# Gate and up of a feed-forward layer made together, a quarter of their products by Strassen's scheme

## The chip, the cores and the metric

The kernel runs on one core of a Trainium2 chip. Its time is the device time of one execution in microseconds (us), and three runs of the kernel before gave a median of 1607.12 us (1605.46 to 1607.89). The core has a matrix engine (TensorE, PE in the profile, with its weight loads shown apart as PEld), a vector engine (VectorE, DVE), a scalar engine (ScalarE, ACT), a general engine (GpSimd, POOL) and a queue engine (SyncE, SP) that issues the transfers. Matrix products are summed in eight PSUM banks of 128 x 512 fp32.

## The reference

One encoder layer on 256 tokens of 2048 features, all in fp32. The stages after the token mixers are

```
h   = layer_norm(ALPHA * h + m @ w_o, ln1_g, ln1_b)
gt, up = split(h @ w_gu, 2)                    # w_gu: 2048 x (2 x 5632)
ffn = (silu(gt) * up) @ w_down                 # w_down: 5632 x 2048
ple = sigmoid(h @ w_pg + b_pg) * (p @ w_pu)
out = layer_norm(ALPHA * h + ffn + ple, ln2_g, ln2_b)
```

Before them stand a first layer norm, one wide projection `h @ w_in`, a gated linear attention over four heads (GLA), a gated spatial mix and the gates that merge the two.

## The kernel before

Every fp32 product is made of three products of fp32r operands: a matrix is split into `hi` (a copy rounded to fp32r, ScalarE, L147) and `lo` (the rest, `raw - hi`, VectorE, L148), and `mm3` (L188 to L190) multiplies xh·wh, xl·wh and xh·wl into one bank. The activations are the stationary operand (128 features x 128 tokens), the weights the moving one (128 features x 512 columns).

The work is one stream of weight chunks. A chunk is two k-tiles (2 x 128 rows) of 512 columns, 512 KB. `pump` walks the stream: before chunk c is used, chunks up to c+5 are loaded and up to c+3 are split, then the chunk's matmuls are issued, then one waiting job (an evacuation or a transposition) is run. A `token_block` makes one block of 512 output columns for both token tiles (2 x 128 tokens) in two banks of the pool `pacc`. A chunk costs 12 matmuls: two k-tiles, two token tiles, three products. Each engine works in order, so a split that is late holds everything behind it on its engine.

In the feed-forward stage 11 gate blocks (`gt`) and 11 up blocks (`up`) alternate, with 8 chunks each. The gate's evacuation is a Silu on ScalarE (L858), the up's a multiplication on VectorE (L868); the result is transposed on TensorE (L282, tile `atp`) and split (L290, L291) to become the stationary operand of the down product. Gate and up come in three parts of 4, 4 and 3 blocks; behind each part stand four down blocks (`dn`) over the part's features, so the last has 12 k-tiles. That last down block is held: the first token tile is finished first, all weights being kept, so that its layer norm (L909, L912, `ln2_out`) can run beside the second tile's matmuls, which are made in two halves of 256 columns.

SBUF is shared by fixed pools: raw chunks, `hi` and `lo` have 4 buffers each (`wp`), eight large slots of 16 KB per partition hold streams and transposed activations (`big`), 7 small tiles (`t2`) the evacuations. PSUM gives 4 banks to blocks (`pacc`) and 4 to transpositions and attention (`paux`).

Of the kernel before, what the change touches and what calls it, by code (L numbers as in the profile page):

```python
# [28 lines left out]
KC = 2  # L29
ET = mybir.EngineType  # L30
# [8 lines left out]
def block_kernel(ctx: ExitStack, tc: tile.TileContext, x, p, ln0_g, ln0_b, w_in, b_in, w_f2, b_f2,  # L39
# [15 lines left out]
    wp = ctx.enter_context(tc.tile_pool(name="wp", bufs=2))  # L55
    big = ctx.enter_context(tc.tile_pool(name="big", bufs=8))
    tmp = ctx.enter_context(tc.tile_pool(name="tmp", bufs=4))
    sm = ctx.enter_context(tc.tile_pool(name="sm", bufs=4))
    pacc = ctx.enter_context(tc.tile_pool(name="pacc", bufs=4, space=bass.MemoryType.PSUM))
    paux = ctx.enter_context(tc.tile_pool(name="paux", bufs=4, space=bass.MemoryType.PSUM))  # L60

    def slot(name, dt=F32):
        return big.tile([P, 4096], dt, tag="big", name=name)

    def t2(name):
        return tmp.tile([P, CB], F32, tag="t2", name=name, bufs=7)

    def tr(name):
        return tmp.tile([P, CB], F32R, tag="t2", name=name, bufs=7)
# [3 lines left out]

    def bcast(src, c0, name, n=CB):
        t = tmp.tile([P, CB], F32, tag="bc", name=name, bufs=4)
        nc.sync.dma_start(t[:, :n], src[c0:c0 + n].partition_broadcast(P))
        return t

# [1 line left out]
    xs = slot("xs").rearrange("p (t d) -> p t d", t=NT)  # L80
    for t in range(NT):
        for c in range(D // XC):
            nc.sync.dma_start(xs[:, t, c * XC:(c + 1) * XC],
                              x[t * P:(t + 1) * P, c * XC:(c + 1) * XC])
# [8 lines left out]
    # vectors that are needed with features on partitions: rows of 128, turned over at once  # L93
# [26 lines left out]
    chunks = []  # L120

    def add_chunk(src, nk, nc_, consume, dst=None):
        chunks.append([src, nk, nc_, consume, None, None, dst])

    G = {}
    jobs = deque()

# [5 lines left out]
    def load(c):  # L133
        src, nk, ncol = chunks[c][:3]
        raw = wp.tile([P, KC * CB], F32, tag="raw", name=f"raw{c}", bufs=4)
        nc.sync.dma_start(raw[:, :nk * ncol].rearrange("p (k c) -> p k c", k=nk), src)
        chunks[c][4] = raw

    def split(c):
        n = chunks[c][1] * chunks[c][2]  # L140
        raw = chunks[c][4]
        if chunks[c][6] is None:
            hi = wp.tile([P, KC * CB], F32R, tag="hi", name=f"hi{c}", bufs=4)
            lo = wp.tile([P, KC * CB], F32R, tag="lo", name=f"lo{c}", bufs=4)
        else:
            hi, lo = chunks[c][6]()
        nc.scalar.activation(hi[:, :n], raw[:, :n], AF.Copy)  # L147
        nc.vector.tensor_tensor(out=lo[:, :n], in0=raw[:, :n], in1=hi[:, :n].bitcast(F32),  # L148
                                op=ALU.subtract)
        chunks[c][5] = (hi, lo)  # L150

    state = {"load": 0, "split": 0, "use": 0}

    def ahead(nload, nsplit):
        while state["load"] < min(nload, len(chunks)):
            load(state["load"])
            state["load"] += 1
        while state["split"] < min(nsplit, len(chunks), state["load"]):
            split(state["split"])
            state["split"] += 1  # L160
# [9 lines left out]
    def consume(c):  # L170
        chunks[c][3](*chunks[c][5])
        state["use"] = c + 1

    def pump(upto=None):
        end = len(chunks) if upto is None else upto
# [16 lines left out]
    def token_block(src, nk, xT, evac, name, held=None, halves=False):  # L192
        """[tokens, CB] = xT.T @ W; evac(t, psum) after the last k. Over the chunks in held the
        first token tile runs ahead of the second, which reads the kept weights. With halves the
        second is finished in two column halves (only with all chunks held)."""
# [4 lines left out]
        def one(i, n, t, c0=0, c1=CB, ps=None):  # L200
            hi, lo = st["w"][i]
            ps = st["ps"][t] if ps is None else ps
            xh, xl = xT() if callable(xT) else xT
            for k in range(n):
                kk = i * KC + k
                xo = kk * S + t * P
                mm3(ps[:, c0:c1], xh[:, xo:xo + P], xl[:, xo:xo + P],
                    hi[:, k * CB + c0:k * CB + c1], lo[:, k * CB + c0:k * CB + c1],
                    kk == 0, kk == nk - 1)
# [4 lines left out]
        def dst(i):  # L214
            def get():
                j = (i - h0_) % 4
                if j == 0:
                    st["keep"] = (slot(f"{name}_kh{i}", F32R), slot(f"{name}_kl{i}", F32R))
                return tuple(x[:, j * KC * CB:(j + 1) * KC * CB] for x in st["keep"])
            return get  # L220

        def mk(i):
            def consume(hi, lo):
                if i == 0:
                    st["ps"] = [pacc.tile([P, CB], F32, tag="acc", name=f"{name}_{t}")
                                for t in range(NT)]
# [11 lines left out]
                elif i == h1_ - 1 and halves:  # L238
                    for j in range(2):
                        ps = st["ps"][1] if j == 0 else pacc.tile([P, CB], F32, tag="acc",  # L240
                                                                  name=f"{name}_1b")
# [9 lines left out]
        for i in range(nchunk):  # L251
            add_chunk(src[:, i * KC:i * KC + size(i), :], size(i), CB, mk(i),
                      dst(i) if h0_ <= i < h1_ else None)

# [1 line left out]
    def rstd_of(var, n, name, eps_scale=None):  # L256
        """(var * scale + eps) ** -0.5 for [P, n]."""
# [27 lines left out]
    def split_to(src, xT, k0, t, eng=nc.vector):  # L285
        xh, xl = xT
        oh = xh.rearrange("p (k s) -> p k s", s=S)[:, k0:k0 + 4, t * P:(t + 1) * P]
        ol = xl.rearrange("p (k s) -> p k s", s=S)[:, k0:k0 + 4, t * P:(t + 1) * P]
# [18 lines left out]
    def ln_turn(src, xT, t, c, key, name):  # L307
        """Normalised rows (t, 512 features from c) to xT with gain and bias."""
        ps = transpose4(src[:, t, c * CB:(c + 1) * CB], f"{name}_ps{t}_{c}")
# [3 lines left out]
    def pair_ps(src, k0, name):  # L313
        """Both token tiles, features of k0 and k0 + 1."""
        ps = aux(f"{name}_ps{k0}")
        for i in range(2):
            for t in range(NT):
                nc.tensor.transpose(ps[:, i * S + t * P:i * S + (t + 1) * P],
                                    src[:, t, (k0 + i) * P:(k0 + i + 1) * P], ident)
# [9 lines left out]
    def pair_split(a, xT, k0):  # L329
        xh, xl = xT  # L330
        sl = slice(k0 * S, (k0 + 2) * S)
        nc.scalar.activation(xh[:, sl], a, AF.Copy)
        nc.vector.tensor_tensor(out=xl[:, sl], in0=a, in1=xh[:, sl].bitcast(F32), op=ALU.subtract)
# [6 lines left out]
    def residual(g, b, c, name):  # L340
        """Gain and bias of the token-major copy, 512 features."""
        gt = bcast(g, c * CB, f"{name}g{c}")
        bt = bcast(b, c * CB, f"{name}b{c}")
        for t in range(NT):
            y = h0[:, t, c * CB:(c + 1) * CB]
# [4 lines left out]
    h0 = xs  # L350
    h0T = (slot("h0Th", F32R), slot("h0Tl", F32R))
# [7 lines left out]
    def keep_busy(n, name):  # L359
        """TensorE's clock rises only while it works."""  # L360
# [12 lines left out]
    def ws_job():  # L373
# [7 lines left out]
        # rows j of chunk 1 do not reach positions i of chunk 0  # L381
# [5 lines left out]
    def v_evac(b):  # L387
        def evac(t, ps):
# [581 lines left out]
```

## Time and profile before

| | before |
|---|---|
| median of three runs | 1607.12 us |
| the profiled execution's span, first to last instruction | 1606.5 us |
| TensorE busy, instructions | 1583.1 us, 7520 |
| VectorE busy | 929.4 us |
| ScalarE busy | 711.6 us |
| mean granted TensorE clock | 0.997 of full speed |

The profile is of one execution. Its span of 1606.5 us is its own time and lies 0.6 us under the median. Busy time of TensorE is modelled from overlapping matmuls (a row of 0.39 us follows another by 0.23 us), so what a matmul costs is read from the starts of successive rows and not from their durations. A few matmul rows can be missing.

### The profile page before, as it was taken

Reading aid. Unit: us, or ns where it says so; the run is one execution under the profiler, and the core shown is the slowest. Engines: PE = TensorE matmul, PEld = TensorE weight load, DVE = VectorE, ACT = ScalarE, POOL = GpSimd, SP = SyncE. Lnnn points to the kernel's source line nnn. Section 1 sums busy time; section 2 is a strip of 40 time slices with the busy share of each in tenths; the row PEclk is TensorE's granted clock in tenths of the full one; section 3 lists DMA queues with packets and bytes.
Section 4 is the critical chain, followed back from the end, with each engine's and each line's share of the span. In section 5 each row is a group of like instructions: output and inputs, shape, how many; then the busy total and the mean of one; then the engine's idle time right before and its main releaser. Section 6 shows DMA issues by size and latency. Waiting matters only on the chain.

```text
span 1606.5 us, 19428 instructions
## 1 busy us (share of the span) xinstructions
PE 1583.1 (99%) x7520; PEld 1329.2 (83%) x7520; DVE 929.4 (58%) x1029; ACT 711.6 (44%) x811; POOL 77.3 (5%) x66
## 2 busy tenths in 40 slices
PE   8999999999999999999999999999999999999996
PEld 7889988888888888888787888888888888888885
DVE  7567555567655556656756554545445455544466
ACT  5445545444444444434534444443444443344432
POOL 1023000001000000000112000000000000000002
PEclk9999999999999999999999999999999999999998
DMA  6776655777777676665576666656666666666663
GB/s 198 237 227 181 198 162 183 210 211 203 216 216 203 204 210 190 196 203 197 164 224 214 199 195 187 193 186 195 195 186 191 189 187 194 196 194 186 190 232 116
DMA packets 164599, 315.45 MB, mean 196 GB/s; under 512 B 10237, under 2 KB 13210, under 8 KB 164250
## 3 DMA queue, kind: packets, MB, share of 16 engines
q1 hardware_dynamic: 164442, 314.19, 65.2%
q8 instruction: 59, 0.97, 0.2%
q14 instruction: 34, 0.28, 0.0%
q10 hardware_dynamic: 64, 0.02, 0.0%
HBM read 312.06 MB, written 2.10 MB: 196 GB/s over the span
## 4 chain that ended last, share of the span: by engine, by line
PE 49%; issue 45%; DVE 2%; DMA 2%; POOL 1%; ACT 1%; SPq 0%; ACTq 0%; POOLq 0%; DVEq 0%
PE og L188 2%; PE v L189 2%; PE ga L190 2%; PE ga L189 2%; PE v L190 2%; PE z L190 2%; PE wo L189 2%; PE u L190 2%; PE z L189 2%; PE gb L190 2%; PE og L190 2%; PE wo L188 2%; PE wo L190 2%; PE ga L188 2%; PE u L188 2%
## 5 line engine op out<-in xcount | busy, mean ns | idle before, releaser
L148 DVE TENSOR_TENSOR lo<-raw,hi 128x1024 fp32r<-128x1024 f32 x542 | 665.4, 1232 | 571.4 <-ACT hi L147 570.5
L147 ACT ACTIVATE hi<-raw 128x1024 fp32r<-128x1024 f32 x542 | 572.5, 1058 | 680.4 <-PE up L189 139.8
L188 PE MATMUL gt<-hi,h1Th 128*128 128x512 f32 x352 | 138.7, 394 | 0.0
L190 PE MATMUL gt<-lo,h1Th 128*128 128x512 f32 x352 | 137.5, 391 | 0.8 <-DVE lo L148 0.8
L189 PE MATMUL gt<-hi,h1Tl 128*128 128x512 f32 x352 | 137.2, 390 | 0.0
L188 PE MATMUL up<-hi,h1Th 128*128 128x512 f32 x352 | 137.1, 389 | 0.0
L190 PE MATMUL up<-lo,h1Th 128*128 128x512 f32 x352 | 137.1, 389 | 0.0
L189 PE MATMUL up<-hi,h1Tl 128*128 128x512 f32 x352 | 137.1, 389 | 0.0
L188 PE MATMUL dn<-hi,acth 128*128 128x512 f32 x328 | 128.3, 391 | 0.0
L190 PE MATMUL dn<-lo,acth 128*128 128x512 f32 x328 | 127.9, 390 | 0.0
L189 PE MATMUL dn<-hi,actl 128*128 128x512 f32 x328 | 127.8, 390 | 0.0
L190 PEld LDWEIGHTS gt<-lo,h1Th 128*128 128x128 f32 x352 | 66.1, 188 | 15.2 <-DVE lo L148 1.3
L190 PEld LDWEIGHTS up<-lo,h1Th 128*128 128x128 f32 x352 | 66.1, 188 | 13.7
L189 PEld LDWEIGHTS up<-hi,h1Tl 128*128 128x128 f32 x352 | 66.1, 188 | 13.7
L188 PEld LDWEIGHTS up<-hi,h1Th 128*128 128x128 f32 x352 | 66.1, 188 | 13.7
L189 PEld LDWEIGHTS gt<-hi,h1Tl 128*128 128x128 f32 x352 | 66.2, 188 | 13.3
L188 PEld LDWEIGHTS gt<-hi,h1Th 128*128 128x128 f32 x352 | 66.2, 188 | 13.1
L190 PEld LDWEIGHTS dn<-lo,acth 128*128 128x128 f32 x328 | 61.6, 188 | 12.8
L188 PEld LDWEIGHTS dn<-hi,acth 128*128 128x128 f32 x328 | 61.6, 188 | 12.7
L189 PEld LDWEIGHTS dn<-hi,actl 128*128 128x128 f32 x328 | 61.6, 188 | 12.6
L265 POOL TENSOR_TENSOR ln_r<-ln_v,mhalf 128x1 f32<-128x1 f32 x6 | 4.2, 693 | 1074.3 <-DVE ln_v L260 1074.3
L188 PE MATMUL ga<-hi,h0Th 128*128 128x512 f32 x128 | 50.4, 394 | 0.0
(269 smaller groups left out, 2843.4 us busy)
## 6 DMA issues: line engine op xcount, KB each, us to landing
raw<-in_w_in_dram SPq DMA_DIRECT2D x226, 512.0 KB, 4.2
raw<-in_w_gu_dram SPq DMA_DIRECT2D x176, 512.0 KB, 3.7
raw<-in_w_down_dram SPq DMA_DIRECT2D x88, 512.0 KB, 3.7
raw<-in_w_o_dram SPq DMA_DIRECT2D x32, 512.0 KB, 3.7
raw<-in_w_pg_dram SPq DMA_DIRECT2D x32, 512.0 KB, 5.0
xs<-in_x_dram SPq DMA_DIRECT2D x4, 512.0 KB, 4.6
raw<-in_w_pu_dram SPq DMA_DIRECT2D x4, 512.0 KB, 4.5
out_dram<-xs SPq DMA_DIRECT2D x8, 256.0 KB, 2.1
```

The source lines that it names most:

```text
L147: nc.scalar.activation(hi[:, :n], raw[:, :n], AF.Copy)
L148: nc.vector.tensor_tensor(out=lo[:, :n], in0=raw[:, :n], in1=hi[:, :n].bitcast(F32), op=ALU.subtract)
L188: nc.tensor.matmul(ps, lhsT=xh, rhs=wh, start=start, stop=False, **kw)
L189: nc.tensor.matmul(ps, lhsT=xl, rhs=wh, start=False, stop=False, **kw)
L190: nc.tensor.matmul(ps, lhsT=xh, rhs=wl, start=False, stop=stop, **kw)
L265: nc.gpsimd.tensor_tensor(out=r[:, :n], in0=v[:, :n], in1=mhalf[:, :n], op=ALU.pow)
```

## The change

Gate and up columns of one j are now one `pair_block`, which reads four quadrants: for a pair of k-tiles, the two token tiles of the activations (2 x 2 blocks with the two k-tiles) times the two k-tiles of gate and up (2 x 2 blocks). For the first two of the eight pairs of k-tiles it uses Strassen's scheme in Winograd's form, 7 block products instead of 8; the other six pairs are made as before. Five banks are used: C11 and C21 (gate, token tiles 0 and 1), C12 and C22 (up), and V for a sum that three of the outputs need.

The scheme's sums of weights are made on VectorE in place in the raw tile (L430, L460, L461) and split like any chunk; the sums of activations are made once (`sums`, tiles `s1`) while `pg` runs. At evacuation each output needs one of three side tiles (`p1`, `p7`, `v`) added, a VectorE addition per output (L1154, L1168).

The memory is laid out anew. One pool of 21 slots of 8 KB takes the place of `wp` and `big`: a slot holds `hi` and `lo` of one chunk, or two raw chunks, or a stream. The numbers of raw and split slots in flight are limited by `limit`. `pacc` has five banks and `paux` three. The parts of the feed-forward are now 3, 3, 3 and 2 blocks, so the last down block has 8 k-tiles, all held. `run_jobs` runs two jobs a step when more than two wait. In the attention the scores' tile `sc` is a small tile that GpSimd clears for each head.

```diff
-    pacc = ctx.enter_context(tc.tile_pool(name="pacc", bufs=4, space=bass.MemoryType.PSUM))
-    paux = ctx.enter_context(tc.tile_pool(name="paux", bufs=4, space=bass.MemoryType.PSUM))
+    pacc = ctx.enter_context(tc.tile_pool(name="pacc", bufs=5, space=bass.MemoryType.PSUM))
+    paux = ctx.enter_context(tc.tile_pool(name="paux", bufs=3, space=bass.MemoryType.PSUM))
...
+    limit = {"raw": 3, "hl": 4}
...
-            ahead(c + 6, c + 4)
-            consume(c)
-            run_jobs(1)
+            while True:
+                if state["split"] <= c or split_ready():
+                    if state["split"] < len(steps):
+                        split_one()
+                        while load_ready():
+                            load_one()
+                        continue
+                break
+            while load_ready():
+                load_one()
+            consume(c)
+            run_jobs(2 if len(jobs) > 2 else 1)
...
+            def split():
+                w = cut(raw.tile[:, :1024], f"{name}_a{i}")
+
+                nc.vector.tensor_tensor(out=r()[:, 0:4:2, :], in0=r()[:, 0:4:3, :],
+                                        in1=r()[:, 2, :].unsqueeze(1).broadcast_to([P, 2, CB]),
+                                        op=ALU.subtract)
+                return w
+
+            def use(w):
+                mul("C11", [X(i, 1, 0)], [W(w, 1)])
+                mul("V", [X(i, 0, 0)], [W(w, 0)])
+                left["C11"] -= 1
...
+            def use(w):
+                mul("C21", [SX(2, i)], [W(w, 1)])
+                mul("C12", [SX(0, i)], [W(w, 0)])
+                if i == s - 1:
+                    p1, p7 = t2(f"{name}_p1"), t2(f"{name}_p7")
+                    nc.scalar.activation(p1, B["V"], AF.Copy)
+                    nc.scalar.activation(p7, B["C21"], AF.Copy)
+                    nc.vector.tensor_tensor(out=p7, in0=p7, in1=B["C12"], op=ALU.add)
+                    st["p1"], st["h"] = p1, p7
...
+            nc.vector.tensor_tensor(out=q(0), in0=q(0), in1=q(3), op=ALU.add)
+            nc.vector.tensor_tensor(out=q(1), in0=q(1), in1=q(0), op=ALU.subtract)
...
+            def use1(w):
+                mul("V", [SX(1, i)], [W(w, 0)])
+                mul("C21", [X(i, 1, 1)], [W(w, 1)])
+                done("C21", 1, 0)
...
+            def use2(w):
+                mul("C12", [SX(3, i)], [(w[:, :CB], w[:, 1024:1024 + CB])])
+                done("C12", 0, 1)
+                if i == s - 1:
+                    v = t2(f"{name}_v")
+                    nc.scalar.activation(v, B["V"], AF.Copy)
+                    st["v"] = v
+                    nc.vector.tensor_tensor(out=st["h"], in0=st["h"], in1=v, op=ALU.add)
...
-        sc = g3[:, 1792 + u * 512:1792 + (u + 1) * 512]
+        sc = t2(f"sc{h}")
+        nc.gpsimd.memset(sc, 0.0)
...
+            if add is not None:
+                u = t2(f"up{j}_{t}")
+                nc.vector.tensor_tensor(out=u, in0=ps, in1=add, op=ALU.add)
+                ps = u
             nc.vector.tensor_tensor(out=a, in0=a, in1=ps, op=ALU.mult)
...
+    s_gu = 2
+    before(len(steps) - 16, lambda: G.update(s1=sums(h1T["x"], s_gu, "s1")))
+    before(len(steps), lambda: limit.update(raw=5, hl=5))
     j = 0
-    for part, npair in enumerate((4, 4, 3)):
+    for part, npair in enumerate((3, 3, 3, 2)):
         k_first = j * 4
         for i in range(npair):
-            token_block(wcols(w_gu, j * CB), KT, h1T_get, gate_evac(j), f"gt{j}")
-            token_block(wcols(w_gu, DFF + j * CB), KT, h1T_get, up_evac(j, part, i * 4), f"up{j}")
+            if s_gu:
+                pair_block((wcols(w_gu, j * CB), wcols(w_gu, DFF + j * CB)), KT, h1T_get,
+                           (gate_evac(j), up_evac(j, part, i * 4)), f"gu{j}", s_gu,
+                           lambda: G["s1"])
...
             token_block(src, npair * 4, lambda part=part: G["act", part], down_evac(b, part == 3),
                         f"dn{part}_{b}", held=(0, 4) if last else None, halves=last)
```

TensorE, the start of the third gate block before (`gt2_0` and `gt2_1` are its banks, `hi326` and `lo326` its first chunk):

```order
L188 MATMUL gt2_0_7746<-hi326_7687,h1Th_6327 128x512
L189 MATMUL gt2_0_7746<-hi326_7687,h1Tl_6328 128x512
L190 MATMUL gt2_0_7746<-lo326_7688,h1Th_6327 128x512
L188 MATMUL gt2_0_7746<-hi326_7687,h1Th_6327 128x512
L189 MATMUL gt2_0_7746<-hi326_7687,h1Tl_6328 128x512
L190 MATMUL gt2_0_7746<-lo326_7688,h1Th_6327 128x512
L188 MATMUL gt2_1_7747<-hi326_7687,h1Th_6327 128x512
```

And in the changed kernel (`gu2_a1` and `gu2_b0` are split steps of the two Strassen pairs, `s1` the activations' sums, `atp1_0` the transposition of the block before):

```order
L393 MATMUL gu2_V_7358<-gu2_a1_s_7296,h1Th0_5971 128x512
L395 MATMUL gu2_V_7358<-gu2_a1_s_7296,h1Tl0_5972 128x512
L397 MATMUL gu2_V_7358<-gu2_a1_s_7296,h1Th0_5971 128x512
L569 MATMUL atp1_0_7379<-ident_81,gt1_0_7327 128x128 x4
L393 MATMUL gu2_C21_7390<-gu2_b0_s_7312,s1_s_6413 128x512
L395 MATMUL gu2_C21_7390<-gu2_b0_s_7312,s1_s_6413 128x512
L397 MATMUL gu2_C21_7390<-gu2_b0_s_7312,s1_s_6413 128x512
L393 MATMUL gu2_C12_7394<-gu2_b0_s_7312,s1_s_6413 128x512
```

The bank now changes after three matmuls in these steps instead of after six, and the transposition of the block before stands after 12 matmuls of the new block, where it stood after 24.

VectorE, the end of up block 1 and the chunks split ahead, before:

```order
L148 TENSOR_TENSOR lo328_7724<-raw328_7685,hi328_7723 128x1024
L868 TENSOR_TENSOR gt1_0_7589<-gt1_0_7589,up1_0_7597 128x512
L868 TENSOR_TENSOR gt1_1_7611<-gt1_1_7611,up1_1_7598 128x512
L148 TENSOR_TENSOR lo329_7743<-raw329_7703,hi329_7742 128x1024
L148 TENSOR_TENSOR lo330_7764<-raw330_7721,hi330_7763 128x1024
L148 TENSOR_TENSOR lo331_7789<-raw331_7740,hi331_7788 128x1024
L291 TENSOR_TENSOR actl0_7426<-atp1_0_7779,acth0_7425 128x4x128
```

The same place in the changed kernel (`raw326` holds the weights of a Strassen pair, whose sums are made in it):

```order
L461 TENSOR_TENSOR raw326_7187<-raw326_7187 128x512
L203 TENSOR_TENSOR gu2_c2_1_s_7365<-raw330_7211,gu2_c2_1_s_7365 128x1024
L1154 TENSOR_TENSOR gt1_0_7327<-gu1_C11_7038,gu1_p1_7103 128x512
L1154 TENSOR_TENSOR gt1_1_7345<-gu1_C21_7074,gu1_v_7244 128x512
L1168 TENSOR_TENSOR up1_0_7348<-gu1_C12_7078,gu1_v_7244 128x512
L1170 TENSOR_TENSOR gt1_0_7327<-gt1_0_7327,up1_0_7348 128x512
L1168 TENSOR_TENSOR up1_1_7362<-gu1_C22_7117,gu1_p7_7104 128x512
L1170 TENSOR_TENSOR gt1_1_7345<-gt1_1_7345,up1_1_7362 128x512
L576 TENSOR_TENSOR act0_1_7384<-atp1_0_7379,act0_1_7384 128x4x128
L203 TENSOR_TENSOR gu2_c3_0_s_7387<-raw332_7238,gu2_c3_0_s_7387 128x1024
```

Two multiplications have become four additions and two multiplications, and the sums of weights stand between the splits ahead of them.

## Rows read from the trace of the kernel before

**Rows 1.** The span and mean granted TensorE clock of the core (cores view).

```profile
core 0: 1606.5 us, clock 0.997
```

**Rows 2.** The page: busy time by engine, and the chain that ended last by engine.

```profile
PE 1583.1 (99%) x7520; PEld 1329.2 (83%) x7520; DVE 929.4 (58%) x1029; ACT 711.6 (44%) x811; POOL 77.3 (5%) x66
...
PE 49%; issue 45%; DVE 2%; DMA 2%; POOL 1%; ACT 1%; SPq 0%; ACTq 0%; POOLq 0%; DVEq 0%
```

**Rows 3.** Stretches of gate/up/down and of the end: busy us (instructions), granted clock, DMA share.

```profile
core 0: us, PE busy (x) PEld busy (x) DVE busy (x) ACT busy (x) POOL busy (x), PEclk, DMA share, GB/s
...
860.00:1540.00 680.00, 679.17 (x3038) 562.16 (x3037) 343.67 (x313) 285.68 (x293) 6.16 (x4) 1.00 0.65 192
1540.00:1606.00 66.00, 53.80 (x272) 45.85 (x270) 44.55 (x60) 18.61 (x18) 8.26 (x6) 0.93 0.49 173
```

**Rows 4.** What TensorE waited for: us in total, times, longest (three rows).

```profile
PE pg L190 <- DVE lo L148: 1.4, 1, 1.4
...
PE pg L188 <- ACT h1Th L290: 1.1, 1, 1.1
...
PE gt L190 <- DVE lo L148: 0.8, 1, 0.8
```

**Rows 5.** Timeline of TensorE in a gate block: start, duration, line, tiles.

```profile
997.01 0.39 PE L188 MATMUL gt<-hi,h1Th 128*128 128x512 f32 x1
...
1002.22 0.39 PE L190 MATMUL gt<-lo,h1Th 128*128 128x512 f32 x1
1002.45 0.60 PE L282 MATMUL atp<-ident,gt 128*128 128x128 f32 x4
1002.80 0.47 PE L188 MATMUL gt<-hi,h1Th 128*128 128x512 f32 x1
```

**Rows 6.** Groups on VectorE: busy us, mean ns, idle time before and its releaser.

```profile
L148 DVE TENSOR_TENSOR lo<-raw,hi 128x1024 fp32r<-128x1024 f32 x542 | 665.4, 1232 | 571.4 <-ACT hi L147 570.5 <-PE z L190 0.3 <-PE sg L190 0.3
...
L868 DVE TENSOR_TENSOR gt<-gt,up 128x512 f32<-128x512 f32 x22 | 15.1, 684 | 0.3
```

**Rows 7.** Groups on ScalarE, same columns.

```profile
L147 ACT ACTIVATE hi<-raw 128x1024 fp32r<-128x1024 f32 x542 | 572.5, 1058 | 680.4 <-PE up L189 139.8 <-PE dn L189 124.4 <-PE gt L189 121.4
...
L290 ACT ACTIVATE acth<-atp 128x512 fp32r<-128x512 f32 x22 | 12.8, 580 | 0.0
```

**Rows 8.** 44 us, about one gate and one up block; columns as in Rows 3.

```profile
951.00:995.00 44.00, 44.00 (x200) 36.42 (x199) 21.96 (x20) 18.71 (x20) 0.00 (x0) 1.00 0.66 190
```

**Rows 9.** Timeline of VectorE, four splits back to back.

```profile
851.52 4.62 DVE L148 TENSOR_TENSOR lo<-raw,hi 128x1024 fp32r<-128x1024 f32 x4
```

**Rows 10.** Timeline around one GLA head's scores.

```profile
219.45 0.68 PE L663 MATMUL sc_ps<-qkT 128*64 128x64 f32 x8
...
220.91 0.63 ACT L668 ACTIVATE sch<-g 128x512 fp32r<-128x512 f32 x1
...
221.65 0.69 DVE L669 TENSOR_TENSOR scl<-g,sch 128x512 fp32r<-128x512 f32 x1 [1.58 <-ACT sch L668]
...
222.91 0.39 PE L188 MATMUL o_ps<-v,sch 128*128 128x512 f32 x1
```

**Rows 11.** Timeline of the end, from the last down block's first token tile.

```profile
1585.00 0.28 PE L188 MATMUL dn<-dn_kh,acth 128*128 128x256 f32 x1
...
1585.20 0.69 DVE L909 TENSOR_TENSOR xs<-xs,dn 128x512 f32<-128x512 f32 x1 [3.82 <-PE dn L190]
...
1593.18 0.41 DVE L909 TENSOR_TENSOR xs<-xs,dn 128x256 f32<-128x256 f32 x1
...
1593.52 0.28 PE L190 MATMUL dn_1b<-dn_kl,acth 128*128 128x256 f32 x1
...
1594.51 0.40 DVE L909 TENSOR_TENSOR xs<-xs,dn_1b 128x256 f32<-128x256 f32 x1
...
1601.92 0.75 DVE L899 SCALAR_TENSOR_TENSOR xs<-xs,ln_r,gb 128x512 f32<-128x512 f32 x1
1603.12 0.38 SPq L903 DMA_DIRECT2D out_dram<-xs  x1
```

More of the change, by code (lines that the diff above doesn't have):

```diff
@@ L117, in col @@
         return cols[name][:n, r0 + i:r0 + i + 1]
-    chunks = []
-    def add_chunk(src, nk, nc_, consume, dst=None):
-        chunks.append([src, nk, nc_, consume, None, None, dst])
+    steps = []
+    halves = []
     G = {}
     jobs = deque()
+    state = {"load": 0, "split": 0, "use": 0, "raw": 0, "hl": 0}
+    limit = {"raw": 3, "hl": 4}
+    pair_open = {}
     def run_jobs(n):
@@ L152, in block_kernel, with __init__, add_half @@
-    state = {"load": 0, "split": 0, "use": 0}
-    def ahead(nload, nsplit):
[L155 to L160, printed above, removed]
+    class Raw:
+        def __init__(self):
+            self.tile, self.left, self.name = None, 0, f"raw{len(halves)}"
+    def add_half(raw, q, src, nk, ncol):
+        halves.append((raw, q, src, nk, ncol))
+        return len(halves)
@@ new lines, in add_step, with add_chunk @@
+    def add_step(split, use, need, free_raw=(), free_hl=None, hl=1):
+        steps.append({"split": split, "use": use, "need": need, "free_raw": free_raw, "hl": hl,
+                      "free_hl": 0, "out": None})
+        i = len(steps) - 1
+        if hl and free_hl is None:
+            steps[i]["free_hl"] += 1
+        return i
+    def add_chunk(src, nk, ncol, consume, free_hl=None):
+        if pair_open:
+            raw, q = pair_open.pop("x"), 1
+        else:
+            raw, q = Raw(), 0
+            pair_open["x"] = raw
+        need = add_half(raw, q, src, nk, ncol)
+        n = nk * ncol
+        def split():
+            return cut(raw.tile[:, q * 1024:q * 1024 + n], f"w{need}", n)
+        return add_step(split, lambda w: consume(w[:, :n], w[:, 1024:1024 + n]), need,
+                        (raw,) if q else (), free_hl)
@@ new lines, in cut, with load_one @@
+    def cut(src, name, n=1024):
+        w = slot(f"{name}_s", F32R)
+        hi, lo = w[:, :n], w[:, 1024:1024 + n]
+        if len(src.shape) == 3:
+            hi, lo = (x.rearrange("p (a c) -> p a c", a=src.shape[1]) for x in (hi, lo))
+        nc.scalar.activation(hi, src, AF.Copy)
+        nc.vector.tensor_tensor(out=lo, in0=src, in1=hi.bitcast(F32), op=ALU.subtract)
+        return w
+    def load_one():
+        raw, q, src, nk, ncol = halves[state["load"]]
+        if raw.tile is None:
+            raw.tile = slot(raw.name)
+            state["raw"] += 1
+        nc.sync.dma_start(raw.tile[:, q * 1024:q * 1024 + nk * ncol].rearrange(
+            "p (k c) -> p k c", k=nk), src)
+        state["load"] += 1
@@ new lines, in load_ready, with split_one, split_ready @@
+    def load_ready():
+        return state["load"] < len(halves) and (
+            halves[state["load"]][0].tile is not None or state["raw"] < limit["raw"])
+    def split_one():
+        st = steps[state["split"]]
+        while state["load"] < st["need"]:
+            load_one()
+        st["out"] = st["split"]()
+        state["hl"] += st["hl"]
+        state["raw"] -= len(st["free_raw"])
+        state["split"] += 1
+    def split_ready():
+        return state["split"] < len(steps) and (
+            state["hl"] + steps[state["split"]]["hl"] <= limit["hl"])
@@ L162, in block_kernel @@
+    def ahead(nload, nsplit):
+        while state["load"] < min(nload, len(halves)):
+            load_one()
+        while state["split"] < min(nsplit, len(steps)):
+            split_one()
     pre = {}
@@ L170, in consume @@
     def consume(c):
-        chunks[c][3](*chunks[c][5])
+        assert c == state["use"] and c < state["split"], (c, state)
+        st = steps[c]
+        st["use"](st["out"])
+        state["hl"] -= st["free_hl"]
         state["use"] = c + 1
     def pump(upto=None):
-        end = len(chunks) if upto is None else upto
+        end = len(steps) if upto is None else upto
         while state["use"] < end:
@@ L673, in gla_out @@
         if h == 0:
[L674 removed]
+            G["ya"] = [slot(f"ya{t}") for t in range(NT)]
         (sh, sl), (vh, vl), ya = G["sc", h], G["v"], G["ya"]
@@ L812, in p_job @@
         nc.vector.tensor_tensor(out=pT[1], in0=ps, in1=pT[0].bitcast(F32), op=ALU.subtract)
-    before(len(chunks) - 16, p_job)
+    before(len(steps) - 16, p_job)
     def pu_evac(b):
```

406 lines of the change are left out of this document (275 added, 131 removed).

## Prediction, made before the changed kernel was run

> **What bounds the kernel now.** I began with the core: the span is 1606.5 us at a granted clock of 0.997 [rows 1], so there is no lower clock to win back. The page then shows one engine busy 99% of the span, TensorE, with VectorE at 58% and ScalarE at 44%; in the chain that ended last TensorE and its issue make up 94% [rows 2]. A share over the span hides stages, so I cut it. From 860 to 1540 us (most of gate, up and down) TensorE is busy 679.17 of 680 us at full clock; VectorE is busy 343.67 us, half of it. Only the end, from 1540 us, has holes: 53.80 of 66 us [rows 3]. The list of waits names no wait of TensorE in gate and up but one of 0.8 us; the 1.4 and 1.1 us in `pg` stand in the stage before [rows 4]. So in the stage that changes TensorE is the bound with nothing to wait for, and the first question is what a matmul costs, the second whether its feeders still keep ahead.
>
> **The matmuls taken out.** Between the starts at 997.01 and 1002.22 us lie 23 matmuls of 512 columns: 5.21 / 23 = 0.2265 us each, across changes of token tile and so of bank; then four transpositions and the slower start behind them take about 0.45 us more per token tile (1002.80 is 0.35 us after 1002.45, and the next regular start comes some 0.1 us late) [rows 5]. A pair of k-tiles costs 8 products x 3 = 24 matmuls before and 7 x 3 = 21 after. Two pairs and 11 blocks: 2 x 3 x 11 = 66 matmuls, 66 x 0.2265 = **-15.0 us**. Per block of gate and up TensorE goes from 192 x 0.2265 + 0.9 = 44.4 us to 43.0 us.
>
> The Trainium skill ("TensorE: Matmul & The Clock Gate", Back-to-back issue gap) gives some 131 ns as the sustained spacing of matmuls of 512 columns between weight loads. By it the 66 would be worth only 8.6 us, an estimate from that page. The rows of this kernel differ: 0.2265 us in every regular row [rows 5], and the measurement decides.
>
> **What VectorE has to do more.** Before, a block of gate and up has 16 splits of 1024 elements (1.232 us each), two multiplications and two activation splits of 0.684 us [rows 6]: 22.4 us, and the window of 44 us shows 21.96 [rows 8]. After, there are 18 splits of 1024 and two of 512, two sums of 2 x 512 (L430), four of 512 (L460, L461), two for `p7`, four additions and two multiplications at evacuation, two activation splits: 20 operations of 1024 and 16 of 512. No row shows L430, which reads strided rows with one operand repeated. The nearest row is the split, also two inputs and 1024 outputs; I take its price, with twice that as the upper end and half as the lower (two of them: 2.5 us, from 1.2 to 4.9). By durations 20 x 1.232 + 16 x 0.684 = 35.6 us; by the spacing back to back, 4.62 / 4 = 1.155 us [rows 9] and the same ratio for the small ones, 33.4 us. That is 78 to 83% of 43.0 us. ScalarE gets 18 x 1.058 + 9 x 0.58 us [rows 7] = 24.3 us, 56%. Neither is the bound on average.
>
> Work in order can still be late at one place, so I laid out the boundary between two blocks, with time 0 at the first matmul of block 2. Splits run some six steps ahead. ScalarE can make `c2_0` only when the slot of `c6_0` is free (-8.2) and `c2_1` when `c6_1` is (-5.4); VectorE then ends `c2_1` at about -2.4. Behind it stand the four additions and two multiplications of block 1, which wait for `C21`, `C12` (done) and `C22` (done at 0): the first multiplication ends at 0.4, the second at 1.8. TensorE wants them for `atp` after 12 matmuls at 2.7 and, for the second, at about 4.5. Slack 2.3 us. Queued behind on VectorE are `c3_0` (ready at 6.3, wanted at 11.7) and the sum that is wanted at 16.8 (`d0`, ready at 9.9). The copies of banks `V` and `C21` and the addition from `C12` end at 3.3, 7.2 and 8.7; TensorE writes `C21` and `C12` again at 8.8 and 10.1. So I cost the extra 13 us of VectorE per block at **0**, the cover being TensorE's 43 us; if the sums cost twice as much, 5 us more before the boundary against 2.3 us of slack leave a wait of 2.7 us.
>
> **The attention.** In a head TensorE ends the scores at 220.13, `sch` is ready at 221.54 and `scl` at 222.34, and `o_ps` begins at 222.91 [rows 10]: 1.4 and 2.2 us of chain, with 12 matmuls (2.7 us) between as cover. With two jobs a step only six stand between, 1.36 us, and `scl` is wanted 0.9 us later. So each of four heads waits 0.1 to 0.3 us; the scores of a head may also wait for copies of the head before behind a split. I take 0.2 x 4 = **+0.8 us**, from 0 to +3.
>
> **The end.** TensorE leaves the first token tile of the last block at 1585.00; VectorE's chain starts at 1585.20, meets the second tile's halves at 1593.18 and 1594.51, and the last transfer goes out at 1603.12 [rows 11]. The second tile's 72 matmuls of 256 columns (1585.00 to 1593.52, 0.12 us each) lie wholly beside this chain. With 8 k-tiles instead of 12 only 48 lie beside it: the other 24, worth 12 of 512 columns, come ahead. VectorE's chain from the first tile's end, 21.3 us, is the same work in the same order. 12 x 0.2265 = **+2.7 us**.
>
> **The rest, at 0.** The new pool changes which split stands before which evacuation at `pg`: its waits of 1.4 and 1.1 us [rows 4] may go or come once more, -2.7 to +3. `sums` is six operations of at most 1024 elements on VectorE, under 7.4 us by the split's price, made once and 16 chunks ahead of their use. A bank changes every three matmuls in the Strassen steps; the rows show no gap where it changes [rows 5]. The start is written out by hand and stays, -1 to +1.
>
> Sum on the profiled execution: 1606.5 - 15.0 + 0.8 + 2.7 = 1595.0 us; that execution lies 0.6 us under the median, so 1595.6 us.
>
> **Rivals.**
> - *VectorE late at the boundary, slower than before.* The sums of weights stand in order ahead of the evacuation (L430, L460, L461), the evacuation ahead of `atp` in TensorE's order. If they and the additions cost twice the split's price, TensorE stands 2.7 us at each of 11 blocks: 1595.6 + 29.7 = 1625 us. It decides from about 1.05 us a block, where 11 of them eat the 11.5 us that are left. For it: VectorE at 83%, with 2.3 us of slack only. Against it: in all rows the price of two-input operations goes with the number of elements, and VectorE's idle time in the window is 22 us [rows 8]. 12%.
> - *Half the gain goes in small waits.* About 0.5 us per block (`C21` or `C12` written again after their copies, with 1.4 us of slack) and +1.5 us in the attention: 1595.6 + 7 = 1603 us. For it: many short slacks; against: none of them is below 1.4 us. 15%.
> - *A gap at each change of bank or a lower clock.* In the Strassen steps some 14 changes per block come after three matmuls instead of six. The granted clock is 1.00, the 2.4 GHz level, through the stage [rows 3], after TensorE had been busy without a hole. If a change cost 0.05 us: 14 x 11 x 0.05 = 7.7, so 1603 us. 4%. The Trainium skill ("TensorE: Matmul & The Clock Gate", A second HAM failure mode: psum-queue depth-cycling) tells of a kernel that cycled through banks, idled briefly between groups and lost its clock again and again; here the trace has changes of bank every six matmuls and no gap, so I give it no more than that.
> - *More than forecast.* The waits at `pg` and the gate's 0.8 us go: 1595.6 - 3.5 = 1592 us, 12%.
>
> **Chances and range.** The forecast itself, 1593.5 to 1599, has 57%. A measurement of this kernel tells 0.2%, 3.2 us, from no change: faster means under 1603.9, slower over 1610.3. The second and third rival lie at the edge of that: most of their 19% is still faster, some 5% within; with the first rival's mild cases 8% are within and 11% slower. The range reaches from the lower ends of the open prices (-2.7 and -1, with VectorE at no cost: 1591) to the middle of the second rival, 1604.
>
> **What the changed profile would show.** Right: 66 fewer full matmuls in gate and up at 0.2265 us; the blocks 43.0 us apart; VectorE 33 to 36 us busy per block and no row of waits of TensorE on `gt` (L1170), `c3` or `p7`; from the end of the last block's first token tile to the end of the span still 21 us. Wrong: a wait of TensorE at `atp` behind the additions, at each block; L430 far above 1.2 us; matmuls of the `gu` groups farther apart than 0.23 us; or a longer wait in `pg` or the attention than in the sum.

## The result, and the profile after

The changed kernel takes 1591.37 us (median of 4 runs, 1591.06 to 1591.90) against 1607.44 us (4 runs) for the kernel before: a ratio of 0.99, 95% interval 0.9889 to 0.9912. It is faster by 16.1 us; 11.5 us were forecast. The cores view and the page's first part of the changed kernel, against [rows 1, 2]:

```profile
core 0: 1589.5 us, clock 0.996
```

```profile
PE 1567.8 (99%) x7442; PEld 1315.6 (83%) x7442; DVE 1062.1 (67%) x1219; ACT 747.1 (47%) x889; POOL 86.5 (5%) x69
```

TensorE has 78 matmul rows fewer: the 66 saved, and at the end 24 of 256 columns became 12 of 512. Its busy share is the same 99%. VectorE rose from 929.4 to 1062.1 us. Most of the gate, up and down blocks, columns as in [rows 3]:

```profile
860.00:1540.00 680.00, 679.99 (x3042) 562.90 (x3041) 473.60 (x495) 337.86 (x377) 0.00 (x0) 1.00 0.59 200
```

TensorE is busy 679.99 of 680 us although VectorE is now busy 473.60 us (70%) instead of 343.67 us. So the added work is hidden in this stretch. The list of TensorE's waits, against [rows 4], is short:

```profile
PE rows_ps L640 <- POOL ln_r L552: 3.9, 1, 3.9
PE busy L647 <- POOL ident masks.py:199: 1.4, 1, 1.4
PE v L277 <- POOL h0Tl L576: 0.9, 1, 0.9
```

All three belong to the start. The waits on splits and on `h1Th` in `pg`, on a split in the gate, and one in `q` are gone.

**Where the 16 us come from.** The starts of four stages on TensorE (start, duration, line, tiles) show it: the first matmul of `og`, of `z`, of `pg` and of the first gate block. Before:

```profile
210.13 0.40 PE L188 MATMUL og<-hi,h0Th 128*128 128x512 f32 x1
...
312.85 0.39 PE L188 MATMUL z<-hi,h0Th 128*128 128x512 f32 x1
...
770.84 0.39 PE L188 MATMUL pg<-pg_kh,h1Th 128*128 128x512 f32 x1
...
863.37 0.39 PE L188 MATMUL gt<-hi,h1Th 128*128 128x512 f32 x1
```

After:

```profile
209.50 0.40 PE L276 MATMUL og<-w_s,h0Th 128*128 128x512 f32 x1
...
312.81 0.39 PE L276 MATMUL z<-w_s,h0Th 128*128 128x512 f32 x1
...
770.79 0.39 PE L276 MATMUL pg<-w_s,h1Th 128*128 128x512 f32 x1
...
859.70 0.39 PE L393 MATMUL gu_C<-gu_a_s,h1Th 128*128 128x512 f32 x1
```

The changed kernel is 0.63 us ahead at `og`, 0.04 us at `z` (the attention between them gave back 0.59 us), 0.05 us at `pg`, and 3.67 us at the first gate block. So `pg` alone gave 3.6 us, before any product had been saved. From the gate's start to the end of the last down block's first token tile it took 1585.00 - 863.37 = 721.63 us before [rows 11] and takes 1568.12 - 859.70 = 708.42 us: 13.21 us less. My two terms for this stretch were -14.95 and +2.72, together -12.23; the other 0.98 us fit the gate's wait that went [rows 4]. Its rows before, with the idle time and its releaser in brackets, are

```profile
874.48 0.39 PE L189 MATMUL gt<-hi,h1Tl 128*128 128x512 f32 x1
875.70 0.50 PE L190 MATMUL gt<-lo,h1Th 128*128 128x512 f32 x1 [0.83 <-DVE lo L148]
```

1.22 us from start to start, 0.99 us more than a matmul costs. The end is as long as before: its rows, against [rows 11], are

```profile
1568.12 0.28 PE L276 MATMUL dn<-w_s,act 128*128 128x256 f32 x1
...
1568.32 0.69 DVE L1210 TENSOR_TENSOR xs<-xs,dn 128x512 f32<-128x512 f32 x1 [3.95 <-PE dn L278]
...
1573.75 0.28 PE L278 MATMUL dn_1b<-w_s,act 128*128 128x256 f32 x1
...
1576.25 0.41 DVE L1210 TENSOR_TENSOR xs<-xs,dn 128x256 f32<-128x256 f32 x1
```

From the first matmul of 256 columns to the end of the span are 21.4 us (21.5 us before). TensorE now ends the second tile at 1573.75, 5.6 us after it began, and VectorE turns to it only at 1576.25.

These pieces add up to the difference of the two spans, 1606.5 - 1589.5 = 17.0 us, and not to the 16.1 us of the medians. In every run on record the time is some 1.8 us longer than the span (1591.31 us against 1589.5 us here). So the profiled execution of the kernel before took about 1608.3 us, an estimate from that difference: 0.9 us above the median of its four runs, and not 0.6 us under it as was said when span and median were compared. The pieces in `pg` and the gate are those of one execution that took longer than the median; by the medians they are somewhat smaller, as the first two experiments show. The forecast does not change by this, since it is the median before less the same 11.5 us.

**The Strassen steps.** Rows of TensorE at the border of two blocks, with the first matmul of two blocks in a row (901.86 and 944.97); in these steps the bank changes after every three matmuls:

```profile
901.86 0.39 PE L393 MATMUL gu_C<-gu_a_s,h1Th 128*128 128x512 f32 x1
...
902.32 0.39 PE L397 MATMUL gu_C<-gu_a_s,h1Th 128*128 128x512 f32 x1
902.54 0.39 PE L393 MATMUL gu_V<-gu_a_s,h1Th 128*128 128x512 f32 x1
...
903.00 0.39 PE L397 MATMUL gu_V<-gu_a_s,h1Th 128*128 128x512 f32 x1
903.22 0.39 PE L393 MATMUL gu_C<-gu_a_s,h1Th 128*128 128x512 f32 x1
...
904.59 0.60 PE L569 MATMUL atp<-ident,gt 128*128 128x128 f32 x4
...
944.97 0.39 PE L393 MATMUL gu_C<-gu_a_s,h1Th 128*128 128x512 f32 x1
```

The blocks lie 43.11 us apart, 43.0 in the prediction. From 902.32 to 903.22 are four matmuls, 0.225 us each, over two changes of bank: no gap. The transposition `atp` stands 12 matmuls into the new block and did not wait. The group of the strided sum on VectorE (columns as in [rows 6]):

```profile
L430 DVE TENSOR_TENSOR raw<-raw 128x1024 f32<-128x1024 f32 x22 | 27.7, 1268 | 0.1
```

The price that no row of before had, L430, is 1.268 us, 3% above the split's 1.232 us that the prediction took for it [rows 6].

### The profile page after: what moved, and what is told of

It is laid out like the page before. It is cut to its first block, busy times and chain, and to the rows that moved or that the text cites. A ratio compares the mean times of both kernels' runs of the same rounds, so it can differ in the third digit from the quotient of the medians.

```text
span 1589.5 us, 19295 instructions
## 1 busy us (share of the span) xinstructions
PE 1567.8 (99%) x7442; PEld 1315.6 (83%) x7442; DVE 1062.1 (67%) x1219; ACT 747.1 (47%) x889; POOL 86.5 (5%) x69
## 4 chain that ended last, share of the span: by engine, by line
PE 49%; issue 46%; DVE 3%; POOL 1%; DMA 1%; ACT 0%; SPq 0%; DVEq 0%; POOLq 0%; ACTq 0%
PE og L276 2%; PE v L277 2%; PE og L278 2%; PE v L278 2%; PE ga L278 2%; PE og L277 2%; PE wo L276 2%; PE z L278 2%; PE ga L277 2%; PE u L278 2%; PE wo L277 2%; PE z L277 2%; PE u L277 2%; PE gb L278 2%; PE gb L277 2%
## 5 line engine op out<-in xcount | busy, mean ns | idle before, releaser
L203 DVE TENSOR_TENSOR w_s<-raw,w_s 128x1024 fp32r<-128x1024 f32 x382 | 463.4, 1243 | 167.8 <-ACT w_s L202 167.4
L202 ACT ACTIVATE w_s<-raw 128x1024 fp32r<-128x1024 f32 x382 | 390.5, 1053 | 221.0 <-PE dn L278 72.4
L393 PE MATMUL gu_C<-gu_c_s,h1Th 128*128 128x512 f32 x528 | 205.4, 389 | 0.0
L395 PE MATMUL gu_C<-gu_c_s,h1Tl 128*128 128x512 f32 x528 | 205.4, 389 | 0.0
L397 PE MATMUL gu_C<-gu_c_s,h1Th 128*128 128x512 f32 x528 | 205.4, 389 | 0.0
L203 DVE TENSOR_TENSOR gu_c_s<-raw,gu_c_s 128x1024 fp32r<-128x1024 f32 x132 | 159.2, 1223 | 60.9 <-ACT gu_c_s L202 60.0
L202 ACT ACTIVATE gu_c_s<-raw 128x1024 fp32r<-128x1024 f32 x132 | 137.9, 1059 | 96.5 <-PE gu_C L397 49.3
L276 PE MATMUL dn<-w_s,act 128*128 128x512 f32 (+1 forms) x352 | 136.9, 389 | 0.0
L278 PE MATMUL dn<-w_s,act 128*128 128x512 f32 (+1 forms) x352 | 136.2, 387 | 0.0
L277 PE MATMUL dn<-w_s,act 128*128 128x512 f32 (+1 forms) x352 | 136.1, 387 | 0.0
L397 PEld LDWEIGHTS gu_C<-gu_c_s,h1Th 128*128 128x128 f32 x528 | 99.1, 188 | 20.6
L393 PEld LDWEIGHTS gu_C<-gu_c_s,h1Th 128*128 128x128 f32 x528 | 99.1, 188 | 20.6
L395 PEld LDWEIGHTS gu_C<-gu_c_s,h1Tl 128*128 128x128 f32 x528 | 99.1, 188 | 20.6
L278 PEld LDWEIGHTS dn<-w_s,act 128*128 128x128 f32 x352 | 66.1, 188 | 13.5
L276 PEld LDWEIGHTS dn<-w_s,act 128*128 128x128 f32 x352 | 66.1, 188 | 13.5 <-ACT act L575 0.3
L277 PEld LDWEIGHTS dn<-w_s,act 128*128 128x128 f32 x352 | 66.1, 188 | 13.3
```

What stands on the lines that cost most here:

```text
L202: nc.scalar.activation(hi, src, AF.Copy)
L203: nc.vector.tensor_tensor(out=lo, in0=src, in1=hi.bitcast(F32), op=ALU.subtract)
L276: nc.tensor.matmul(ps, lhsT=xh, rhs=wh, start=start, stop=False, **kw)
L277: nc.tensor.matmul(ps, lhsT=xl, rhs=wh, start=False, stop=False, **kw)
L278: nc.tensor.matmul(ps, lhsT=xh, rhs=wl, start=False, stop=stop, **kw)
L393: nc.tensor.matmul(ps, lhsT=xh, rhs=wh, start=first and j == 0, stop=False, skip_group_check=True)
```

## The experiments

All are compared with the changed kernel's 1591.37 us or with runs of the kernel before made beside them.

**No Strassen pair.** `s_gu = 0` and the call of `sums` left out, all else as changed.

```diff
-    s_gu = 2
-    before(len(steps) - 16, lambda: G.update(s1=sums(h1T["x"], s_gu, "s1")))
+    s_gu = 0
```

> The changed kernel with the pool, the parts 3, 3, 3, 2 and the order of steps of the change, but gate and up as separate blocks with all eight products (no Strassen pair). My sum: the 66 matmuls come back at 0.2265 us each, so 1591.4 + 15.0 = 1606.4 us (1605 to 1607.5), about 1 us under the kernel before, because the waits in pg that went (some 3.5 us) outweigh the longer end (2.7 us). Rival, the 66 matmuls are worth 131 ns each: 1600 us. Rival, the waits in pg went because of the pair block: 1610 us.

Measured 1606.24 us (1605.97 to 1606.72, 11 runs), ratio to before 0.9992, interval 0.9983 to 1.0001. The 66 matmuls are worth 1606.24 - 1591.37 = 14.87 us, 0.2253 us each; the rival price of 131 ns falls. The waits in `pg` are gone here too (the first gate matmul starts at 859.71), so they went with the pool and its steps and not with the pair block. Taken alone, the rest of the change is not told from no change. By the medians it is 1.2 us better; with the end's 2.83 us (next run) all that lies ahead of the end gave about 4.0 us, where the two traces show 4.8 us (17.0 - 14.95 + 2.72).

**The last down block with 12 k-tiles again.**

```diff
-    for part, npair in enumerate((3, 3, 3, 2)):
+    for part, npair in enumerate((2, 3, 3, 3)):
...
+                before(len(steps), lambda: limit.update(hl=8))
...
-                        f"dn{part}_{b}", held=(0, 4) if last else None, halves=last)
+                        f"dn{part}_{b}", held=(0, 6) if last else None, halves=last)
```

> The changed kernel with parts 2, 3, 3, 3, so that the last down block has 12 k-tiles again, all held. My term for the end: 24 matmuls of 256 columns more stand beside VectorE's layer norm of the first token tile, so -2.7 us: 1588.7 us (1588 to 1589.5). Rival, the end is set by something else than the first token tile's end (the held splits, gb2's load): 1591.4 us or more.

Measured 1588.54 us (1588.39 to 1588.57), 2.83 us less than the changed kernel. The timeline of its end:

```profile
1565.32 0.28 PE L276 MATMUL dn<-w_s,act 128*128 128x256 f32 x1
...
1565.52 0.69 DVE L1210 TENSOR_TENSOR xs<-xs,dn 128x512 f32<-128x512 f32 x1 [6.67 <-PE dn L278]
```

VectorE's chain starts at the first tile's end as before, and TensorE's second tile now fills 8.5 us beside it. The term for the end, +2.7 us, is shown by this run, which also moves one gate and up block from the first part to the last.

**The kernel before, with `b_pg` fetched early.** Prompted by the list of VectorE's waits, where `a_pg` waits for that transfer; for the tile `b_pg` before, the idle time in front of its users and what ended it:

```profile
  DMA b_pg<-in_b_pg_dram: 18.8, 4
```

and in the changed kernel, where the first of these transfers is asked for at 784.7 and used at 793.3, no user waits for the transfer:

```profile
  PE pg L278: 0.5, 1
```

TensorE's rows in `pg` before, with the idle time and its releaser in brackets:

```profile
777.89 0.40 PE L190 MATMUL pg<-pg_kl,h1Th 128*128 128x512 f32 x1
779.40 0.50 PE L188 MATMUL pg<-pg_kh,h1Th 128*128 128x512 f32 x1 [1.11 <-ACT h1Th L290]
780.13 0.50 PE L189 MATMUL pg<-pg_kh,h1Tl 128*128 128x512 f32 x1 [0.23 <-DVE h1Tl L291]
...
850.99 0.39 PE L189 MATMUL pg<-hi,h1Tl 128*128 128x512 f32 x1
852.80 0.50 PE L190 MATMUL pg<-lo,h1Th 128*128 128x512 f32 x1 [1.42 <-DVE lo L148]
853.13 0.39 PE L188 MATMUL pg<-hi,h1Th 128*128 128x512 f32 x1
```

```diff
+    def early_bias(b):
+        bias_t[f"pg{b}"] = bcast(b_pg, b * CB, f"b_pg{b}")
...
+        before(len(chunks) - 5, lambda b=b: early_bias(b))
```

> The kernel before with one edit: the broadcast of b_pg is asked for five chunks before the end of its pg block instead of at the evacuation. If the waits of TensorE at 850.99 (1.58 us) and 874.48 us (0.99 us) come from VectorE standing at a_pg for this transfer (18.8 us of idle VectorE in four waits), both go: 1607.4 - 2.6 = 1604.9 us. Rival, they come from the order of the splits behind it alone: 1607.4 us, and the two waits stay.

Measured 1605.10 us (1604.26 to 1606.97, 11 runs) against 1607.46 us: ratio 0.9986, interval 0.9978 to 0.9995. TensorE's waits in `pg` in this run:

```profile
PE pg L188 <- ACT h1Th L290: 0.4, 1, 0.4
PE pg L189 <- DVE h1Tl L291: 0.2, 1, 0.2
```

The wait on a split at 852.80 and that of the gate are gone, as forecast, and the interval is clear of no change. The waits on `h1Th` and `h1Tl` stay, the first with 0.4 us instead of 1.1 us.

**The kernel before, with fewer splits ahead around the first `pg` block.**

```diff
-            ahead(c + 6, c + 4)
+            ahead(c + 6, c + (2 if -6 <= c - G.get("n_pu", 10 ** 6) < 2 else 4))
```

> The kernel before with one edit: around the first pg block chunks are split two steps ahead instead of four, so that VectorE makes the transposed activations (h1t, L297) before the kept splits of pg (pg_kl, three in a row before). If the two waits of TensorE at 777.89 and 779.40 us (1.28 and 0.50 us) come from these splits standing ahead: both go, 1607.5 - 1.8 = 1605.7 us. Rival, ScalarE's h1Th is late by itself: the waits stay, 1607.5 us; or splits that are now late cost the same again.

Measured 1607.19 us (1604.42 to 1608.29, 11 runs), ratio 0.9993, interval 0.9984 to 1.0002: not told from no change. In its profiled execution the waits are

```profile
PE gt L190 <- DVE lo L148: 0.6, 1, 0.6
...
PE pg L188 <- ACT h1Th L290: 0.4, 1, 0.4
```

so the wait on `h1Th` is 0.4 us instead of 1.1 us. But the run before this one has the same 0.4 us without this edit, so that the edit made it shorter is not shown. The profiled execution was the fastest of the 11 (1604.42 us), and its `pg` is 3.0 us shorter than before (770.12 to 859.64, against 770.84 to 863.37) though the median moved by 0.25 us: single traces of the kernel before and its variants differ by as much as the effect. Inconclusive.

**Both edits together.** The diffs are those of the last two.

> The kernel before with both edits, b_pg asked for early and fewer splits ahead around the first pg block. If these two causes make up what the new pool saved in pg: pg's excess goes from 4.1 to about 0.5 us and the gate's first wait (0.8 us) goes too, 1607.5 - 4.0 = 1603.5 us (1602.8 to 1604.5). If the splits ahead cost nothing of their own, as the time of that edit alone (1607.2) says, 1605 us.

Measured 1604.20 us (1603.70 to 1605.69, 11 runs) against 1607.18 us: ratio 0.9984, interval 0.9975 to 0.9993. That is 3.0 us, within the expected span. In its profiled execution `pg` takes 89.45 us (770.95 to 860.40), against 92.53 us before and 88.91 us in the changed kernel, and the gate's wait is gone. So both edits together account for 3.0 of the about 4.0 us that the changed kernel gained ahead of the end by the medians. The early transfer is shown as a cause (2.4 us alone). That the splits ahead are another is not shown: 0.3 us alone, and 0.6 us between this run and the early transfer alone, are within the scatter of the runs.

**More work on VectorE.** Reads of a raw tile whose result nobody uses, behind L430 in each `a` step (two such steps in a block); with 4 and with 8 reads a step.

```diff
+                for m in range(4):
+                    jk = sm.tile([P, 1, 6], F32, tag="jk", name=f"{name}_jk{i}_{m}", bufs=2)
+                    nc.vector.bn_stats(out=jk[:, 0, :], in_=raw.tile[:, :CB])
                 return w
```

> The changed kernel with eight more VectorE reads of 512 elements (statistics of a raw tile that nobody uses, 0.68 us each) in each block of gate and up, in order behind the sums L430: 5.5 us more in a block, as if the sums of weights cost twice. My rival forecast that 5 us more there cost TensorE 2.7 us a block (1620 us). The run with three pairs, which adds 4.5 us of real work and hid it all, speaks for less: 1591 to 1596 us. If the work is hidden to the last, 1591.4 us.

Measured 1591.17 us (1590.94 to 1591.45): no change. The reads themselves (columns as in [rows 6]) are 4.9 us a block by busy time:

```profile
L435 DVE BATCH_NORM_STATS2 gu_jk<-raw 128x6 f32<-128x512 f32 x88 | 54.0, 677 | 0.1
```

At the border of blocks 1 and 2 the first multiplication, and the transposition on TensorE that wants it, are

```profile
945.44 0.68 DVE L1173 TENSOR_TENSOR gt<-gt,up 128x512 f32<-128x512 f32 x1
...
947.56 0.60 PE L572 MATMUL atp<-ident,gt 128*128 128x128 f32 x4
```

The slack is 1.4 us, where the changed kernel has 2.4 us (border rows in the section on the prediction). The reads moved the multiplication by 1.0 us only, because VectorE's waits in front of the border are gone and because the four small sums of the next block (L460, L461 of the changed kernel), which stood ahead of it, stand behind it in this run's order. So the run shows that this much more work costs nothing, and not quite what 5 us ahead of the border would do in the old order.

> The same with sixteen reads, 11 us more in each block: VectorE would need 33 + 11 = 44 to 46 us where TensorE needs 43, so VectorE is the bound: at least 1 to 3 us in each of 11 blocks, 1602 to 1624 us, with waits of TensorE on splits (L203) or on gt (L1170). If the work still hides, it was not the average that would decide: 1591 us.

Measured 1596.26 us (1595.98 to 1596.43): 4.9 us more, between the two expectations. The reads, and the waits of TensorE in gate and up:

```profile
L435 DVE BATCH_NORM_STATS2 gu_jk<-raw 128x6 f32<-128x512 f32 x176 | 105.9, 676 | 0.1
...
PE gu_C L397 <- DVE gu_b_s L203: 1.6, 3, 0.5
...
PE gu_C L393 <- DVE gu_p L456: 0.5, 1, 0.5
```

and 43 us with one of these waits in them (columns as in [rows 3]), in which VectorE is busy 41.93 us:

```profile
1053.00:1096.00 43.00, 42.37 (x186) 34.49 (x185) 41.93 (x53) 23.53 (x26) 0.00 (x0) 1.00 0.62 200
...
1060.32 0.49 PE L397 MATMUL gu_C<-gu_b_s,s_s 128*128 128x512 f32 x1 [0.53 <-DVE gu_b_s L203]
```

The four waits stand at 869.63, 1060.32, 1256.33 and 1452.31: in the first gate and up block, and in the first one behind each stage of down blocks. In front of the one at 1060.32 VectorE has worked without a wait since 1043.02. So somewhere between 4.9 and 9.6 us a block beyond the change VectorE begins to decide, first where a part begins. The list shows 2.1 us, while the start-to-start excess of the `gu` matmuls rose by some 5 us; the first three blocks are 0.7, 0.4 and 0.1 us longer than in the changed kernel, so part of the cost is spread in pieces that the list doesn't name. The expected cost was too high: it had added durations to 44 to 46 us, but rows back to back overlap (16 reads of 0.68 us in 9.58 us).

**Three Strassen pairs.**

```diff
-    s_gu = 2
+    s_gu = 3
```

> The changed kernel with three Strassen pairs of the eight instead of two: 33 matmuls fewer (-7.5 us), and VectorE gets some 4.5 us more in each block, about 38 of 42.4 us. If the slack at the boundary (VectorE's first multiplication ends 2.3 us before TensorE wants it, and it idles 0.6 to 2 us before it) is enough: 1584 us. If VectorE's order decides at the boundary: up to 2 us of wait in each of 11 blocks at atp or at the first c step, 1584 to 1606 us, with rows of waits of TensorE on gt (L1170) or on the splits.

Measured 1583.74 us (1583.60 to 1583.79): 7.63 us less than with two, for 33 matmuls (0.231 us each). 42 us of it, about one block:

```profile
904.00:946.00 42.00, 42.00 (x191) 34.84 (x190) 35.14 (x40) 24.73 (x29) 0.00 (x0) 1.00 0.59 201
```

TensorE is full and VectorE at 84%: the cover that hid the work of two pairs hides that of three.

**One job a step.** `run_jobs(1)` in place of `run_jobs(2 if len(jobs) > 2 else 1)`.

> The changed kernel with one waiting job run after each step instead of two, so that 12 matmuls stand again between a head's scores and its output. My term for the attention: the stretch of og, scores and outputs is 0.6 us longer in the changed kernel's trace than before, so without it 1591.4 - 0.6 = 1590.8 us (1590.4 to 1591.2). Rival, the jobs of the pair block pile up and the evacuations come late: over 1592 us.

Measured 1591.11 us (1590.95 to 1591.34): 0.26 us less, and the runs overlap with those of the changed kernel (1591.06 to 1591.90), so by the time it is not told from no change. In the trace of the changed kernel six `og` matmuls stand between a later head's scores and its output:

```profile
227.60 0.74 PE L276 MATMUL o_ps<-v,sch 128*128 128x512 f32 x2
228.18 0.40 PE L276 MATMUL og<-w_s,h0Th 128*128 128x512 f32 x1
```

From 226.06 on six `og` matmuls run; with the slow first one they end their turn at 227.55, the output's first two begin at 227.60, and the next `og` follows at 228.18, 0.58 us for two where 0.45 is regular. That is some 0.2 us in a head, as forecast. With one job a step the first matmuls of `og` and `z` are

```profile
209.25 0.40 PE L276 MATMUL og<-w_s,h0Th 128*128 128x512 f32 x1
...
311.97 0.39 PE L276 MATMUL z<-w_s,h0Th 128*128 128x512 f32 x1
```

so this stretch takes 102.72 us as in the kernel before, against 103.31 us in the changed kernel (and 103.29 to 103.33 us in the runs without Strassen, with the larger last block and with three pairs). The attention's 0.59 us are gone, as expected. But from the first gate block to the end of the last block's first token tile this run takes 708.89 us (858.86 to 1567.75) instead of 708.42: the other order gives 0.47 us back there.

**Both gains together.** Three pairs and parts 2, 3, 3, 3.

> Both edits together, three Strassen pairs and parts 2, 3, 3, 3: if the two gains lie at different places they add: 1583.7 - 2.8 = 1580.9 us (1580 to 1582). If the larger last part is paid back by VectorE's order there: 1583 us.

Measured 1581.28 us (1580.91 to 1581.39, 5 runs), ratio to before 0.9835, interval 0.9822 to 0.9849. This version beats both kernels, by 26.2 and 10.1 us.

## Why the prediction was right, and where its size was off

The measured 1591.37 us lie in the stated range, 0.4 us from its lower end, and outside the forecast's own 1593.5 to 1599. That it still lies in the range is in part luck. By the two terms that the prediction names, the lower end would be 1595.6 - 2.7 - 1 = 1591.9 us, above the measured time; 1591 takes the attention at nothing as well, where the trace has it at +0.59 us. The term that did come, in `pg`, went past its own lower end.

- *TensorE is the bound, and a matmul costs 0.2265 us.* Right: 14.87 us without Strassen against the sum's 15.0, and 7.63 us for the next 33. The rows of the timeline decided against 131 ns, the sustained spacing that the Trainium skill ("TensorE: Matmul & The Clock Gate", Back-to-back issue gap) gives.
- *The extra work of VectorE costs nothing.* Right, and for the reason given. At the border of blocks 1 and 2 its rows are

```profile
943.81 0.69 DVE L1168 TENSOR_TENSOR up<-gu_C,gu_v 128x512 f32<-128x512 f32 x1 [0.56 <-PE gu_C L397]
944.61 0.69 DVE L1170 TENSOR_TENSOR gt<-gt,up 128x512 f32<-128x512 f32 x1
```

and TensorE's transposition of the first tile starts at

```profile
947.70 0.60 PE L569 MATMUL atp<-ident,gt 128*128 128x128 f32 x4
```

  The first multiplication (L1170) ends at 945.30, 0.33 us behind the block's first matmul (0.4 in the prediction) and 2.4 us before it is wanted (2.3 in the prediction). VectorE had even idled 0.56 us for a bank before it. In one block of 43 us it is busy

```profile
904.00:947.00 43.00, 43.00 (x195) 35.60 (x194) 33.68 (x36) 23.25 (x27) 0.00 (x0) 1.00 0.57 196
```

  33.68 us, between the forecast 33.4 and 35.6. The rival of a late VectorE did not come: L430 costs 1.268 us and not twice the split's price, and TensorE waits at no border. Its price of 2.7 us a block for 5 us more work is not borne out by the added reads either, 4.9 us a block that cost nothing, with the one difference in order told there. What the rival's price left out: work put in front of a point where VectorE waits first uses up that wait.
- *The end, +2.7 us.* Right: +2.83 by experiment.
- *The attention, +0.8 us.* 0.59 us in the trace between `og` and `z`, and gone there with one job a step; the time as a whole moved by 0.26 us only, within the scatter.
- *A gap at each change of bank, a lower clock.* Neither: four matmuls over two changes in 0.90 us, granted clock 1.00 in the middle stretch, the 2.4 GHz level.
- *The rest, at 0.* This is the term that was mis-sized. I had its lower end, -2.7 us, from TensorE's list of waits, and took 0; in the traces it was -3.6 in `pg` and -1.0 in the gate, by the medians about -4.0 for all ahead of the end. Two things were missed. The list counts 1.4 and 1.1 us, while the start to start of those rows shows 1.58 and 1.28 us more than a matmul: idle time is counted from the modelled end of the row before, 0.39 us behind its start, where the next regular start comes after 0.2265 us, so each wait is counted 0.16 us short. The first matmul after a wait is slow as well: the next start comes 0.33 us behind it (852.80 to 853.13), 0.10 us more than regular. And I did not follow the waits back: VectorE's list showed 18.8 us at `a_pg` for the broadcast of `b_pg`, and behind it on VectorE stood the splits that TensorE wanted. I had left that list out. In the changed kernel `a_pg` no longer waits for that transfer. The early transfer alone gave 2.4 us and, with fewer splits ahead, 3.0 us; what the remaining 1 us is stays open. My rival "more than forecast", 1592 us at 12%, is the case that came.

## What to carry to other kernels

Where the matrix engine is full, a product saved is worth its start-to-start spacing in the timeline; the work that it puts on other engines can cost nothing: here VectorE was busy up to 36 of 43 us at no cost, and with 41 to 42 of 43 us in two of three blocks it cost 0.45 us a block. Follow each wait of the bound engine back, through the in-order queue of the engine it names, to the transfer at its head, before a change that reorders transfers is costed at zero. Read the price of a wait from the starts of the rows, and compare medians too, since one trace is one execution. Look at what the last block leaves beside the final chain: here a smaller last block cost 2.8 us.

## What the runs showed of the hardware that was not expected

The kernel before spreads over 3 to 5 us from run to run (1605.69 to 1609.49 us in 21 runs), the changed one over 0.8 us, and the changed one without Strassen pairs over 0.8 us too. The cause is open. The waits for `b_pg` are not the whole of it: the kernel before with that transfer early still spreads over 2.7 us. In its trace VectorE still waits 15.7 us in all for transfers of other biases (33.4 us with `b_pg` in the kernel before, 3.0 us in the changed one); whether the spread comes from these was not tried. It shows in single traces: `pg` takes 88.89 to 88.92 us in those of the changed kernel and of its runs without Strassen, with the larger last block and with three pairs, but 92.53 us in that of the kernel before and 89.52 us in that of the variant with fewer splits ahead, whose medians differ by 0.25 us.
